# Moving every float32r operand of a two-layer block from 192 to 128 modulo 512 bytes of SBUF

## The chip, the cores and the metric

The kernel runs on one core of one Trainium2 chip. The metric is the device time of one execution in microseconds, as the median of several runs. A core has a matrix engine (TensorE, PE in the profile, its weight loads PEld), a vector engine (VectorE, DVE), a scalar engine (ScalarE, ACT), GpSimd (POOL) and SyncE (SP), which here only issues DMAs. Data lives in SBUF, a memory of 128 partitions; an address below is a byte offset inside a partition, the same in all 128. Matmul results go to PSUM.

## What is computed

Two transformer layers over one sequence of 512 tokens and 1024 features, all in float32. Layer 0 mixes tokens with HGRN2 (a gated linear recurrence in chunks), layer 1 with three groups of dilated window attention; each mixer is followed by a SwiGLU network with 2816 hidden features. Six modulation vectors a layer come from a small condition `c`.

```python
def reference(x, c, positions, ada_w, ada_b, norm_g, hgrn_w_in, ...):
    cond = jax.nn.silu(c)
    ...
    h = x
    for layer in range(DEPTH):
        mod = (cond @ ada_w[layer] + ada_b[layer])[:, None, :]
        sh1, sc1, g1, sh2, sc2, g2 = jnp.split(mod, 6, axis=-1)
        u = rms_norm(h, norm_g[layer, 0]) * (1.0 + sc1) + sh1
        ...
            y = hgrn2_mixer(u, ...) or dilated_attention_mixer(u, ...)
        h = h + (1.0 + g1) * rms_norm(y, norm_g[layer, 1])
        u = rms_norm(h, norm_g[layer, 2]) * (1.0 + sc2) + sh2
        y = swiglu_ffn(u, ffn_w_in[layer], ffn_w_out[layer])
        h = h + (1.0 + g2) * rms_norm(y, norm_g[layer, 3])
    return h
```

## The kernel before

**Float32 from three float32r products.** The kernel computes its large products with operands of the type float32r. It splits each operand `a` of a large product into a high part (`hi`, a cast to float32r, on ScalarE) and a low part (`lo` = `a` - `hi`, on VectorE), and sums three products. That is the helper `three`, whose three lines carry nearly all matmuls of the profile:

```python
def three(ps, ah, al, bh, bl, start, stop):
    pe.matmul(ps, ah, bh, start=start, stop=False)   # L431
    pe.matmul(ps, ah, bl, start=False, stop=False)   # L432
    pe.matmul(ps, al, bh, start=False, stop=stop)    # L433
```

The first operand is stationary (128 x 128, loaded by a LDWEIGHTS ahead of each matmul), the second is the moving one (128 partitions x 512 or 256 columns). In a row of the profile `out<-a,b` has the moving operand as `a` and the stationary one as `b`.

**Weights.** The class `Stream` brings weight tiles of 128 x 2048 floats from HBM (`raw`, two buffers, DMAs on SyncE's queue) and splits them into `hi` and `lo` (three buffers each; `hiq` and `loq` are the same places under another name).

**Where float32r operands stand in SBUF.** Tiles are taken from pools that are stacked from the left end or from the right end of SBUF, in the order in which the pools open. `base`, the first pool from the left, holds `h`, `ident`, `ones`, `shared` and, at its end, `uh` and `ul`, the two parts of the normed activations. Then come `raw`, `hi` and `lo`. All of `uh`, `ul`, `raw`, `hi` and `lo` start at 192 modulo 512 bytes, and every slice that a matmul takes of them begins at a multiple of 512 bytes from there. Three groups of tiles in later pools are brought to a place by a pad tile that nothing reads or writes: `apart` (attention's reordered activations, left) by 96 floats and `oh` of the mixers' outputs (right) by 72 floats, both to 192 modulo 512; and `th`, `tl` by 112 floats. The last two lie behind the two `spare` tiles, which start at 192 and are 6144 bytes long each, so 12288 + 448 bytes further: at 128 modulo 512. The first products' two `late` tiles, from the right, lie at 448. `oT`, whose places also serve as `ol`, and the FFN's `oh` and `ol` lie at 192.

**The stages**, in the order of time (us of the span): modulation and the value product of HGRN, 0 to 77; HGRN heads with their gates, to 265; its output product and the turn into the FFN, to 344; FFN of layer 0, to about 695 (plain blocks, then `seven_products`, then the output product); attention with `seven_values`, to about 1130; its output product and the turn, to 1202; FFN of layer 1, to the end.

`seven_products` computes the FFN's input product of one block of 128 hidden features (gate and up together) with seven block products instead of eight, Strassen's scheme. Each of the seven (`run`) is 4 x 3 matmuls of 256 columns; three take slices of `uh` and `ul` as the moving operand, four take slices of `th` and `tl`, which hold sums and differences of such slices. There are 16 blocks in layer 0 and 18 in layer 1. `seven_values` does the same for four attention value products, with the activations stationary and `hiq`, `loq` moving. `block` is the plain form (24 matmuls of 512 columns, or, in the turns, two halves of 256).

The order of instructions on each engine is written out by hand around the turns and in the seven products; elsewhere a scheduler orders them. Attention's small matmuls (`qk`, `ident`, `V`, `state` and the like) read float32 operands.

Of the kernel before, what the change touches and what calls it, by code (L numbers as in the profile page):

```python
# [9 lines left out]
F32 = mybir.dt.float32  # L10
# [5 lines left out]
P = 128  # L16
# [138 lines left out]
def block_kernel(tc, x, c, positions, ada_w, ada_b, norm_g, hgrn_w_in, lower, hgrn_norm_g, hgrn_w_out,  # L155
# [6 lines left out]
    R4 = lambda a: a.rearrange("p (r l) -> p l r", r=4)  # L162

    with ExitStack() as ctx:
        base = ctx.enter_context(tc.tile_pool(name="base", bufs=1))
        wp = ctx.enter_context(tc.tile_pool(name="weights", bufs=1))
        psum = ctx.enter_context(tc.tile_pool(name="psum", bufs=1, space=bass.MemoryType.PSUM))
        dpool = ctx.enter_context(tc.tile_pool(name="scratch", bufs=1, space=bass.MemoryType.DRAM))
# [6 lines left out]
        def fresh(p, shape, tag, bufs=1, dt=F32):  # L175
            uid[0] += 1
            return p.tile(shape, dt, name=f"{tag}{uid[0]}", tag=tag, bufs=bufs)
# [257 lines left out]
        def block(whi, wlo, c0, width, ps=None, tok=slice(0, S), kts=range(KT), u=(uh, ul)):  # L435

            ps = bank("mm") if ps is None else ps
            for kt in kts:
                a = kt * width + c0
                three(ps[:, tok], whi[:, a:a + P], wlo[:, a:a + P], u[0][:, kt, tok], u[1][:, kt, tok], kt == 0, kt == KT - 1)  # L440
            return ps
# [304 lines left out]
        def token_sums(th, tl, room, uh=uh, ul=ul):  # L746


            q = lambda a, k: a[:, k // 2 * 4:k // 2 * 4 + 4, k % 2 * 256:k % 2 * 256 + 256].bitcast(F32)
            t = [room[:, 2 * k:2 * k + 2].rearrange("p a (b n) -> p (a b) n", b=2) for k in range(4)]  # L750
            for k in (0, 1, 3, 2):
                dve.tensor_add(t[k], q(uh, k), q(ul, k))
            dve.tensor_sub(t[0], t[0], t[1])
            dve.tensor_sub(t[1], t[3], t[1])
            dve.scalar_tensor_tensor(t[3], t[0], -1.0, t[3], op0=OP.mult, op1=OP.subtract)
            dve.scalar_tensor_tensor(t[2], t[3], -1.0, t[2], op0=OP.mult, op1=OP.subtract)

            def cut():
                for k in (3, 0, 2, 1):
                    act.copy(th[:, k], t[k])  # L760
                    dve.tensor_sub(tl[:, k], t[k], th[:, k].bitcast(F32))
            return cut
# [132 lines left out]
        def ffn(l, first, close, nxt, side):  # L895
            turns.close()
            close()
            with ExitStack() as fx:
# [4 lines left out]
                with ExitStack() as qx:  # L903
                    sgp = qx.enter_context(tc.tile_pool(name=f"sg{l}", bufs=1, side=side))
                    qp = qx.enter_context(tc.tile_pool(name=f"quarters{l}", bufs=1, side=bass.opposite_side(side)))
                    spare = [qp.tile([P, 3 * 512], F32R, name=f"spare{l}{k}") for k in range(2)]
                    qp.tile([P, 112], F32, name=f"pad_q{l}")
                    th = qp.tile([P, 4, 4, 256], F32R, name=f"th{l}")
                    tl = qp.tile([P, 4, 4, 256], F32R, name=f"tl{l}")
                    for j in range(PLAIN[l]):  # L910
                        if j == 0:
                            pss = first
                        else:
                            pss = []
                            for i in range(2):
                                w = st.take()
                                pss += [block(*w, k * P, 256) for k in range(2)]
                        sg = [fresh(sgp, [P, S], "sg", 2) for _ in range(2)]
                        for k in range(2):
                            act.activation(sg[k], pss[k], AF.Silu)  # L920
                        if j == 0:
                            cut = token_sums(th, tl, midt[:, NF - 8:])
                        for k in range(2):
                            dve.tensor_mul(mid(2 * j + k), pss[2 + k], sg[k])
                        if j == 0:
                            cut()
                            fixed.close()
                    seven_products(range(2 * PLAIN[l], NF), mid, sgp, spare, th, tl)
# [415 lines left out]
        qp = cx.enter_context(tc.tile_pool(name="h_q", bufs=1))  # L1344
# [268 lines left out]
        def open_attention():  # L1613
# [20 lines left out]
            return v_prod  # L1634

        ffn(0, first, h0.close, ((1, 0), open_attention), "right")
        v_away = dpool.tile([P, NT, 512], F32, name="v_away")

# [195 lines left out]
        for kind, g, i in order:  # L1834
# [22 lines left out]
            for k in range(2):  # L1857
# [9 lines left out]
                7: [back(3)]}  # L1867
        first = mixer_out(oT, store[0], (3, 5), gates.pop((1, 2)), 1, "left", cx.close, tail)
        ffn(1, first, hx.close, None, "right")


# [29 lines left out]
```

## Time and profile before

| | |
|---|---|
| median of 3 runs | 1519.1 us (1518.32 to 1520.51) |
| profiled execution, its own time | 1520.42 us |
| its span, first to last instruction | 1518.7 us |
| granted TensorE clock | 0.997 |
| busy: PE, PEld, DVE, ACT, POOL | 99%, 87%, 70%, 47%, 15% |
| moved by DMA | 199.14 MB, mean 131 GB/s |
| matmuls | 9231 |

Matmuls are pipelined: one starts before the one ahead of it has ended, so their durations overlap, and the ends are modelled. The spacing of their starts, read from the timeline, is what each one costs in a train without gaps. Busy shares count overlapped time once.

### The profile page before, as it was taken

Reading aid. Unit: us, or ns where it says so; the run is one execution under the profiler, and the core shown is the slowest. Engines: PE = TensorE matmul, PEld = TensorE weight load, DVE = VectorE, ACT = ScalarE, POOL = GpSimd, SP = SyncE. Lnnn points to the kernel's source line nnn. Section 1 sums busy time; section 2 is a strip of 40 time slices with the busy share of each in tenths; the row PEclk is TensorE's granted clock in tenths of the full one; section 3 lists DMA queues with packets and bytes.
Section 4 is the critical chain, followed back from the end, with each engine's and each line's share of the span. In section 5 each row is a group of like instructions: output and inputs, shape, how many; then the busy total and the mean of one; then the engine's idle time right before and its main releaser. Section 6 shows DMA issues by size and latency. Waiting matters only on the chain. (4 is left out here: it accounts for less than half of the span.)

```text
span 1518.7 us, 23536 instructions
## 1 busy us (share of the span) xinstructions
PE 1501.0 (99%) x9231; PEld 1316.2 (87%) x9231; DVE 1061.3 (70%) x1837; ACT 719.0 (47%) x1215; POOL 235.2 (15%) x208
## 2 busy tenths in 40 slices
PE   8999999999999999999999999999999999999998
PEld 6777888898999988888987888988888899999886
DVE  4577767486888897476667766686466978888633
ACT  4433443363454433375545666356655544454231
POOL 1012211031222211140001110011002212221100
PEclk9999999999999999999999999999999999999999
DMA  9554444125333356423166540365213333334521
GB/s 308 171 175 132 160 139 167 56 84 166 112 106 104 106 196 227 152 103 125 57 194 169 149 129 29 116 190 140 83 53 116 102 94 111 112 105 147 199 106 56
DMA packets 206943, 199.14 MB, mean 131 GB/s; under 512 B 6840, under 2 KB 164720, under 8 KB 206576
## 3 DMA queue, kind: packets, MB, share of 16 engines
q1 hardware_dynamic: 203856, 190.87, 40.7%
q10 hardware_dynamic: 1952, 6.65, 1.2%
q8 instruction: 72, 1.18, 0.3%
q0 software_dynamic: 1024, 0.13, 0.2%
q14 instruction: 39, 0.32, 0.1%
HBM read 192.31 MB, written 5.31 MB: 130 GB/s over the span
## 5 line engine op out<-in xcount | busy, mean ns | idle before, releaser
L88 DVE TENSOR_TENSOR lo<-raw,hi 128x2048 fp32r<-128x2048 f32 x68 | 158.8, 2336 | 94.3 <-ACT hi L87 94.1
L87 ACT CAST hi<-raw 128x2048 fp32r<-128x2048 f32 x68 | 129.8, 1908 | 193.6 <-DMA raw<-in_ffn_w_out_dram 55.6
L431 PE MATMUL ps_mm<-apart,hi 128*128 128x512 f32 x384 | 151.4, 394 | 0.0
L432 PE MATMUL ps_mm<-apart,hi 128*128 128x512 f32 x384 | 151.2, 394 | 0.0
L433 PE MATMUL ps_mm<-apart,lo 128*128 128x512 f32 x384 | 150.7, 394 | 0.0
L431 PE MATMUL ps_mm<-uh,hi 128*128 128x512 f32 (+1 forms) x400 | 146.3, 366 | 0.0
L432 PE MATMUL ps_mm<-ul,hi 128*128 128x512 f32 (+1 forms) x400 | 144.3, 361 | 1.0 <-DVE ul L531 1.0
L433 PE MATMUL ps_mm<-uh,lo 128*128 128x512 f32 (+1 forms) x400 | 144.5, 361 | 0.0
L814 ACT CAST hiq<-raw 128x1024 fp32r<-128x1024 f32 x68 | 68.4, 1051 | 66.1 <-DVE raw L802 65.1
L431 PE MATMUL ps_mm<-hi,oh 128*128 128x512 f32 x240 | 94.0, 392 | 0.0
L432 PE MATMUL ps_mm<-lo,oh 128*128 128x512 f32 x240 | 93.4, 389 | 0.0
L431 PEld LDWEIGHTS ps_mm<-uh,hi 128*128 128x128 f32 x400 | 75.5, 189 | 19.7 <-issue 8.4
L432 PEld LDWEIGHTS ps_mm<-ul,hi 128*128 128x128 f32 x400 | 75.6, 189 | 12.1 <-DVE ul L531 1.4
L433 PEld LDWEIGHTS ps_mm<-uh,lo 128*128 128x128 f32 x400 | 75.5, 189 | 11.5
L433 PEld LDWEIGHTS ps_mm<-apart,lo 128*128 128x128 f32 x384 | 72.2, 188 | 14.9 <-DVE lo L88 0.3
L432 PEld LDWEIGHTS ps_mm<-apart,hi 128*128 128x128 f32 x384 | 72.2, 188 | 14.2
L431 PEld LDWEIGHTS ps_mm<-apart,hi 128*128 128x128 f32 x384 | 72.2, 188 | 14.0
L250 DVE SCALAR_TENSOR_TENSOR shared<-raw,cond,shared 128x512 f32<-128x512 f32 x98 | 73.3, 748 | 10.6 <-DMA raw<-in_ada_w_dram 9.7
L818 DVE TENSOR_TENSOR loq<-raw,hiq 128x1024 fp32r<-128x1024 f32 x68 | 80.0, 1218 | 0.4 <-ACT hiq L814 0.4
L252 POOL PARTITION_ALL_REDUCE shared<-shared x14 | 45.9, 3280 | 203.5 <-DVE shared L250 203.5
L798 POOL TENSOR_TENSOR raw<-raw 128x512 f32<-128x512 f32 x34 | 54.6, 1607 | 104.5 <-DVE loq L794 47.3
L802 DVE TENSOR_TENSOR raw<-raw 128x1024 f32<-128x1024 f32 x34 | 41.7, 1226 | 39.1 <-POOL raw L798 39.1
(448 smaller groups left out, 4393.9 us busy)
## 6 DMA issues: line engine op xcount, KB each, us to landing
raw<-in_ada_w_dram SPq DMA_DIRECT2D x40, 1024.0 KB, 5.2
raw<-in_ffn_w_in_dram SPq DMA_DIRECT2D x136, 256.0 KB, 3.6
raw<-in_attn_w_in_dram SPq DMA_DIRECT2D x48, 512.0 KB, 5.3
raw<-in_ffn_w_out_dram SPq DMA_DIRECT2D x22, 1024.0 KB, 4.9
raw<-in_hgrn_w_in_dram SPq DMA_DIRECT2D x12, 1024.0 KB, 5.5
raw<-in_attn_w_in_dram SPq DMA_DIRECT2D x12, 1024.0 KB, 5.2
raw<-in_ffn_w_in_dram SPq DMA_DIRECT2D x10, 1024.0 KB, 5.1
first<-in_ada_w_dram SPq DMA_DIRECT2D x14, 512.0 KB, 7.4
```

Source lines behind the costliest of these rows:

```text
L87: self.nc.scalar.copy(hi, t)
L88: self.nc.vector.tensor_sub(lo, t, hi.bitcast(F32))
L250: dve.scalar_tensor_tensor(a, r[:, k], sc, a, op0=OP.mult, op1=OP.add)
L252: pool.partition_all_reduce(a, a, P, bass.bass_isa.ReduceOp.add)
L431: pe.matmul(ps, ah, bh, start=start, stop=False)
L432: pe.matmul(ps, ah, bl, start=False, stop=False)
L433: pe.matmul(ps, al, bh, start=False, stop=stop)
L798: pool.tensor_add(r[:, 2], r[:, 2], r[:, 0])
L802: dve.tensor_tensor(r[:, 0:2], r[:, 0:3:2], r[:, 1:2].broadcast_to((P, 2, 512)), op=OP.add)
L814: act.copy(hi, src)
L818: dve.tensor_sub(lo, src, hi.bitcast(F32))
```

## The change

Two pads are added and one grows. `shift_r` (16 floats, 64 bytes) is the first tile from the right end, so every tile of the right stack moves down by 64 bytes. `shift_l` (112 floats, 448 bytes) is the first tile of `base`, so every tile of the left stack moves up by 448 bytes. Both are -64 modulo 512. `pad_q` grows from 112 to 128 floats, so that `th` and `tl` move up by 512 bytes and stay at 128 modulo 512. The stationary and the moving operands of all float32r matmuls then start at 128 modulo 512, with the two `late` tiles at 384. Float32 tiles and the targets of the DMAs move along. No instruction is added, taken away or moved.

```diff
     with ExitStack() as ctx:
+        ctx.enter_context(tc.tile_pool(name="shift", bufs=1, side="right")).tile([P, 16], F32, name="shift_r")
         base = ctx.enter_context(tc.tile_pool(name="base", bufs=1))
+        base.tile([P, 112], F32, name="shift_l")
         wp = ctx.enter_context(tc.tile_pool(name="weights", bufs=1))
...
                     spare = [qp.tile([P, 3 * 512], F32R, name=f"spare{l}{k}") for k in range(2)]
-                    qp.tile([P, 112], F32, name=f"pad_q{l}")
+                    qp.tile([P, 128], F32, name=f"pad_q{l}")
                     th = qp.tile([P, 4, 4, 256], F32R, name=f"th{l}")
                     tl = qp.tile([P, 4, 4, 256], F32R, name=f"tl{l}")
```

## The prediction

> **What bounds the kernel.** I read the page's busy lines and its slices first, then the waits of TensorE.
>
> ```profile
> span 1518.7 us, 23536 instructions
> PE 1501.0 (99%) x9231; PEld 1316.2 (87%) x9231; DVE 1061.3 (70%) x1837; ACT 719.0 (47%) x1215; POOL 235.2 (15%) x208
> PEclk9999999999999999999999999999999999999999
> ```
> ```profile
> PE ps_mm L1128 <- DVE cols L1158: 1.9, 1, 1.9
> PE ps_b L1819 <- ACT h L1797: 1.5, 2, 1.1
> PE ps_b L1212 <- POOL expo L195: 1.2, 1, 1.2
> PE ps_b L512 <- DVE xn L506: 1.2, 2, 0.6
> ```
>
> TensorE is busy for 99% of the span at the full granted clock, and its worst wait in the whole program is 1.9 us. (Columns of the second view: total us, times, longest.) So the program lasts as long as its matmuls take to follow each other, and a change that touches no instruction can only matter through that spacing. The durations do not show it, since matmuls overlap; the starts do. Here are the first and the last row of three unbroken trains, from the timeline (start us, duration us, line, tiles).
>
> ```profile
> 1402.97 0.39 PE L433 MATMUL ps_b<-hi,ol 128*128 128x512 f32 x1
> ...
> 1494.09 0.39 PE L433 MATMUL ps_a<-hi,ol 128*128 128x512 f32 x1
> ```
> ```profile
> 317.78 0.28 PE L431 MATMUL ps_mm<-uh,hi 128*128 128x256 f32 x1
> ...
> 319.22 0.28 PE L431 MATMUL ps_mm<-uh,hi 128*128 128x256 f32 x1
> ```
> ```profile
> 387.59 0.28 PE L431 MATMUL ps_mm<-th,hiq 128*128 128x256 f32 x1
> ...
> 390.99 0.28 PE L431 MATMUL ps_mm<-th,hiq 128*128 128x256 f32 x1
> ```
>
> The tile behind the arrow that comes first is the moving operand, the second the stationary one. Between the two rows lie 402, 12 and 30 matmuls. Spacing: 91.12 us / 402 = 226.7 ns for 512 columns; 1.44 / 12 = 120.0 ns for 256 columns of `uh`; 3.40 / 30 = 113.3 ns for 256 columns of `th`. From the first two, 256 columns cost 226.7 - 120.0 = 106.7 ns, and a fixed 13.3 ns comes on top of every matmul whose moving operand lies at 192. For `th` and `tl` the fixed part is 113.3 - 106.7 = 6.7 ns. These two are the only float32r tiles that lie at 128 modulo 512 already (448 bytes behind `spare`, which lies at 192). Their stationary operands lie at 192, as everywhere. The difference is not in one train only:
>
> ```profile
> L431 PEld LDWEIGHTS ps_mm<-th,hiq x204: 187/188/192, 387.1 to 1380.7; 128*128 128x128 f32 x102
> L431 PE MATMUL ps_mm<-th,hiq x204: 276/276/286, 387.2 to 1380.8; 128*128 128x256 f32 x102
> L431 PEld LDWEIGHTS ps_mm<-uh,spare x136: 187/192/192, 382.8 to 1376.5; 128*128 128x128 f32 x136
> L431 PE MATMUL ps_mm<-uh,spare x136: 278/283/283, 383.0 to 1376.7; 128*128 128x256 f32 x136
> L431 PE MATMUL ps_mm<-hiq,uh x96: 282/283/365, 739.5 to 989.3; 128*128 128x256 f32 x96
> L1190 PE MATMUL ps_mm<-late,uh x16: 389/389/397, 60.0 to 74.5; 128*128 128x512 f32 x16
> ```
>
> (Durations are least/median/greatest, by tile.) In every train a duration is the spacing plus 163 ns: 276 for `th`, 283 for `uh`, and 283 again where `hiq` moves, whose slices follow each other in the tile exactly as those of `th` do. So the walk through the tile is not what sets `th` apart; the start address is what is left. `late` lies at 448, and its 389 ns are the 0.39 of the train at 192.
>
> **The change, part by part.** Counts are from the loops. With 512 columns: 192 (first values) + 576 (24 blocks of HGRN) + 2x192 (both mixers' outputs) + 288 (12 plain FFN blocks) + 2x528 (FFN outputs) + 192 (two value products) + 1152 (48 query and key blocks) = 3840. With 256 columns at 192: 34x36 in the seven products, 4x168 in the seven values, 384 halves = 2280. With 256 columns at 128 (`th`, `tl`): 34x48 = 1632.
>
> 1. The left pad (448 bytes) lifts every left tile, the right pad (64 bytes) lowers every right tile: modulo 512 each falls by 64. No instruction is added, removed or moved, on any engine or queue; the pads are never read or written. Cost of the pads themselves: 0 of time and 576 bytes of room with the next item. The tightest place is in the FFN, where `tl` ends 864 bytes below `sg`; 288 are left, so no new pair of tiles shares bytes there.
> 2. `pad_q` grows by 64 bytes, so that `th` and `tl` stay at 128 while all else comes down to them. For them only the distance to their stationary operand changes, from -64 to 0.
> 3. Moving operands go from 192 to 128. I take the fixed part of `th`: 13.3 to 6.7 ns. 512 columns: 3840 x 6.67 = 25.6 us. 256 columns: 2280 x 6.67 = 15.2 us. `th`: 0. Together -40.8 us. The bounds are below and above nothing: if the distance of the two operands is what counts, this term is 0 and item 2 costs 1632 x 6.67 = +10.9; if the fixed part falls to what the half-rate float32 matmuls pay, it is larger. Their row:
>
> ```profile
> L1725 PE MATMUL ps_a<-qk,qk 128*128 128x256 f32 x48 | 11.7, 380 | 0.0
> ```
>
> 380 - 163 = 217 ns for 256 columns at twice 106.7, a fixed part of about 4 ns. From 6.7 to 4 on all 7752 matmuls would be another 21 us, -62 in all. I take -40.8, because `th` is the same engine mode, width and stationary tile.
> 4. Stationary operands also go from 192 to 128. No row shows a float32r load from another offset. The loads of `th` and of `uh` come from the same tiles and take 188 and 192 ns, 4 ns apart, so I take 0; the ends are those of item 3.
> 5. Float32 operands (`h`, `ident`, `qk`, `V`) move too, by 64 bytes. I take 0: the two groups below read `ident` and `h` at 128 and `qk` at 320, and their means lie 1 ns apart.
> ```profile
> L1792 PE MATMUL ps_a<-ident,h 128*128 128x128 f32 x120 | 18.4, 274 | 0.7 <-DVE h L1780 0.7
> L1743 PE MATMUL ps_a<-qk,qk 128*128 128x128 f32 x128 | 17.0, 275 | 0.2 <-DVE h L1799 0.2
> ```
>
> 6. ScalarE, VectorE and the DMAs write the moved tiles. The nearest rows write the same shape to 128 (`th`) and to 192 (`hiq`): 1045 and 1052 ns on ScalarE. That is 0.7% of an engine that is 47% busy: 0. Of the DMAs no row compares two offsets; TensorE's waits above name none of them, so 0 again.
>
> ```profile
> L760 ACT CAST th<-mid x8: 1041/1045/1053, 344.4 to 1202.1; 128x1024 fp32r<-128x1024 f32 x8
> L814 ACT CAST hiq<-raw x68: 1041/1052/1060, 378.3 to 1379.3; 128x1024 fp32r<-128x1024 f32 x68
> ```
>
> What can be late once TensorE is faster? By stage (us, PE, PEld, DVE, ACT busy, counts in brackets):
>
> ```profile
> 0.00:90.00 90.00, 85.31 (x485) 63.99 (x486) 45.35 (x90) 40.40 (x60) 5.85 (x16) 0.96 0.79 235
> 380.00:530.00 150.00, 150.00 (x1280) 149.46 (x1280) 126.91 (x137) 71.75 (x91) 34.86 (x30) 1.00 0.37 106
> 820.00:1140.00 320.00, 317.50 (x1786) 275.69 (x1787) 210.51 (x617) 185.56 (x379) 34.28 (x33) 1.00 0.40 116
> ```
>
> In the seven products one column block takes 36 x 120.0 + 48 x 113.3 = 9760 ns; it would take 84 x 113.3 = 9520, and VectorE needs 126.91/150 of 9760 = 8260. It stays covered. In attention VectorE has 66%. In the first 90 us the DMAs are 79% busy and other waits set the pace: I count the 192 matmuls there as lost, 1.3 us. Around the four turns between mixer and FFN, TensorE waits for `xn` and the like, through short chains that do not run through its own matmuls; some 200 matmuls a turn, half of their gain lost, is 4 x 200 x 6.67 / 2 = 2.7 us. Hence -40.8 + 1.3 + 2.7 = -36.8. The profiled execution took 1520.4 us (its span 1518.7), 1.3 above the median of the runs, 1519.1. Sum: 1520.4 - 36.8 = 1483.6, or about 1482 against that median.
>
> [...]
>
> **Rivals.**
> - *Distance, not place.* The stream of the moving operand and the load of the next stationary one run at the same time and get in each other's way when they start at the same offset; `th` is fast because it lies 64 bytes below its weights. Then all else keeps 13.3 ns, `th` and `tl` go from 6.7 to 13.3, and the kernel becomes slower by 1632 x 6.67 = 10.9 us: 1530. It decides once the distance explains four fifths of the effect (40.8 / (40.8 + 10.9) = 0.79). For it: the load takes 192 ns beside `uh`, 188 beside `th`. Against it: a matmul without any load beside it is no shorter.
>
> ```profile
> 87.94 0.39 PE L432 MATMUL ps_mm<-ul,hi 128*128 128x512 f32 x1
> 87.94 0.19 PEld L433 LDWEIGHTS ps_mm<-uh,lo 128*128 128x128 f32 x1
> 88.16 0.39 PE L433 MATMUL ps_mm<-uh,lo 128*128 128x512 f32 x1
> 88.48 0.16 PEld L228 LDWEIGHTS ps_mm<-raw,cond_tiles 128*32 128x32 f32 x8 [0.35 <-issue]
> ```
>
>   The matmul at 87.94 has a load beside it from its start, that at 88.16 none for 320 ns; both last 0.39. Without the 13.3 ns the second would show 0.38. Ends of matmuls are modelled, so this is no proof.
> - *Only the narrow ones.* The 13.3 ns of 512 columns is due to something else, only 256 columns gain: -15.2 us, 1504. For it: no 512-column row at 128 exists. Against: the fixed part is the same for both widths at 192.
> - *More falls away.* Aligned loads as well: -62 us, 1457.
> [...]
>
> **How the numbers follow.** Chances: the forecast 0.60 with a range of its own of 1474 to 1490 (all 40.8 us gained, or a further 8 lost to waits); only the narrow 0.08; more 0.06; nothing 0.12; distance 0.14. The range 1468 to 1523 leaves out "more" and "distance", 0.20. About 0.2%, 3 us, can be told from no change here; faster 0.60 + 0.08 + 0.06 = 0.74, same 0.12, slower 0.14.
>
> **What would show it.** Right: 512-column trains at 220.0 ns spacing (duration 382 to 383), `uh` with 256 columns at 113.3 (276), `th` still 276, loads at 188 beside all of them, the seven products at 9.52 us a block, TensorE still 98 to 99% busy. Wrong: `th` at 283 and 389 unchanged (distance), 389 unchanged with 276 everywhere (only the narrow), or the spacing as forecast but TensorE idle for much more than the 17.7 us of now (1518.7 - 1501.0).

## The result, and the profile after

The changed kernel takes 1529.0 us (1528.4 to 1531.5), against 1519.1 before: ratio 1.0067, 95% interval 1.0050 to 1.0084. It became slower by about 10 us where 37 us less were forecast. The rival "distance, not place" had named 1530. The profiled execution took 1528.4 us.

The page's busy lines and one window in the seven products of layer 0 (us, then PE, PEld, DVE, ACT, POOL busy, counts in brackets):

```profile
span 1526.7 us, 23536 instructions
PE 1510.1 (99%) x9231; PEld 1326.0 (87%) x9231; DVE 1064.4 (70%) x1837; ACT 718.4 (47%) x1215; POOL 235.1 (15%) x208
```
```profile
380.00:530.00 150.00, 150.00 (x1246) 149.73 (x1245) 123.34 (x133) 68.78 (x87) 34.30 (x29) 1.00 0.37 106
```

TensorE is as busy as before and waits for nothing new; its longest wait is 2.0 us, at the same place. But the 150 us of the window now hold 1246 matmuls where there were 1280, at the same granted clock of 1.00. 150/1246 is 120.4 ns a matmul, 150/1280 was 117.2. The lines by tile say which ones became slower (least/median/greatest ns):

```profile
L433 PEld LDWEIGHTS ps_mm<-th,hiq x204: 192/192/192, 385.7 to 1388.2; 128*128 128x128 f32 x102
L433 PE MATMUL ps_mm<-th,hiq x204: 283/283/283, 385.8 to 1388.4; 128*128 128x256 f32 x102
L433 PE MATMUL ps_mm<-uh,spare x136: 278/283/284, 381.5 to 1384.0; 128*128 128x256 f32 x136
L433 PE MATMUL ps_mm<-hiq,uh x96: 282/283/365, 743.1 to 992.1; 128*128 128x256 f32 x96
```

`uh` and `hiq` moved from 192 to 128 and kept their 283 ns. `th` stayed at 128 and went from 276 to 283, its load from 188 to 192, without the least spread. The starts agree (timeline; from the first row to the second it is 35, 23 and 402 matmuls):

```profile
385.84 0.28 PE L433 MATMUL ps_mm<-th,hiq 128*128 128x256 f32 x1
...
390.04 0.28 PE L435 MATMUL ps_mm<-th,loq 128*128 128x256 f32 x1
```
```profile
390.16 0.28 PE L433 MATMUL ps_mm<-uh,hiq 128*128 128x256 f32 x1
...
392.92 0.28 PE L435 MATMUL ps_a<-uh,loq 128*128 128x256 f32 x1
```
```profile
1410.92 0.39 PE L435 MATMUL ps_b<-hi,ol 128*128 128x512 f32 x1
...
1502.04 0.39 PE L435 MATMUL ps_a<-hi,ol 128*128 128x512 f32 x1
```

4.20/35 = 120.0 ns for `th` (113.3 before), 2.76/23 = 120.0 for `uh` (120.0 before), 91.12/402 = 226.7 for 512 columns (226.7 before). A block of the seven products takes 10.08 us from its start to the next where it took 9.76; for 34 blocks that is 10.9 us. Summed over the whole trace, from each start to the next, the float32r matmuls of 256 columns take 474.5 us where they took 463.7, those of 512 columns 896.2 where they took 897.7. That is +10.8 and -1.6 (with rounding) of the span's +7.9; the last -1.3 lies among the float32 matmuls and the waits. Of the +10.8, `th` and `tl` have 9.6; the rest is `uh` and the others.

### The profile page after: what moved, and what is told of

Read it like the earlier page. It is cut to its first block, busy times and chain, and to the rows that moved or that the text cites. A ratio compares the mean times of both kernels' runs of the same rounds, so it can differ in the third digit from the quotient of the medians.

```text
span 1526.7 us, 23536 instructions
## 1 busy us (share of the span) xinstructions
PE 1510.1 (99%) x9231; PEld 1326.0 (87%) x9231; DVE 1064.4 (70%) x1837; ACT 718.4 (47%) x1215; POOL 235.1 (15%) x208
## 5 line engine op out<-in xcount | busy, mean ns | idle before, releaser
L433 PEld LDWEIGHTS ps_mm<-apart,hi 128*128 128x128 f32 x384 | 72.2, 188 | 14.1
```

## The experiments

**Place or distance.** In the kernel before, `th` differs from `uh` in two things: its place (128, not 192) and its distance from its weights (-64 bytes, not 0). The change took the place to all and the distance from `th`. Two kernels part them. The first is the changed kernel with the old `pad_q`: all operands at 128, `th` and `tl` at 64.

```diff
-                    qp.tile([P, 128], F32, name=f"pad_q{l}")
+                    qp.tile([P, 112], F32, name=f"pad_q{l}")
```

> The changed kernel with the pad of th and tl back at 112 floats: th and tl at 64, everything else float32r at 128 modulo 512. Distance theory (what counts is the start of the moving operand minus that of the stationary operand being loaded beside it): the distance is -64 again, th at 276 ns duration and 113.3 ns spacing, 1519 us, the same as before. Place theory (a moving operand at 128 is fast only against loads at 192, or a multiple of 128 bytes is what helps): 64 is no such place, th stays at 283 ns, 1529 us.

Measured: 1519.7 us, ratio to before 0.9995 (0.9987 to 1.0004). `th` is fast again, at 64:

```profile
L433 PE MATMUL ps_mm<-th,hiq x204: 276/276/286, 385.8 to 1380.0; 128*128 128x256 f32 x102
```

The second is the kernel before with the new `pad_q` and nothing else: `th` and `tl` at 192 like their weights.

```diff
-                    qp.tile([P, 112], F32, name=f"pad_q{l}")
+                    qp.tile([P, 128], F32, name=f"pad_q{l}")
```

> The kernel before with the pad of th and tl alone grown from 112 to 128 floats: th and tl at 192, distance 0, nothing else moved. Distance theory: the whole loss of the change comes back, th at 283 ns, 1632 x 6.67 = 10.9 us more, 1529 us. If the loss came from the shift of the other tiles (float32 operands, DMA targets, writes of the other engines): 1519 to 1522 us.

Measured: 1531.5 us, ratio 1.0073 (1.0060 to 1.0086).

```profile
L431 PE MATMUL ps_mm<-th,hiq x204: 283/283/315, 386.5 to 1390.4; 128*128 128x256 f32 x102
```

The whole loss is in the 16 floats added to `pad_q`. The two big pads, which move everything else, do nothing that can be measured. Place is ruled out.

**What a distance costs.** The next kernel holds nothing but trains of 72 matmuls, the moving operand at every 16 bytes (512 columns: every 32) from 256 below to 256 above its stationary one; the granted clock is 1.0.

> Matmuls alone, in trains of 72, that compute no part of the reference: float32r, 256 and 512 moving columns, the stationary operand at 0 modulo 512 and the moving one at each distance from -256 to +256 in steps of 16 bytes (32 for 512 columns). Distance theory: 283 and 389 ns at 0 and at +-256 (late against uh), 276 and 382 at -64; the other distances are open, and one value for both widths at each distance is expected. If only the narrow ones can gain, wide trains stand at 389 at every distance.

The groups of this kernel, by train (busy us, mean ns of one). A train's spacing is its busy time less one duration, over 71; the starts, from the 21st on, give the figure to 0.1 ns.

```profile
L49 PE MATMUL wide_m000above<-M,W 128*128 128x512 f32 x72 | 16.5, 389 | 0.0
L49 PE MATMUL wide_m064above<-M,W 128*128 128x512 f32 x72 | 16.6, 391 | 0.0
L49 PE MATMUL wide_m064below<-M,W 128*128 128x512 f32 x72 | 17.0, 395 | 0.0
L49 PE MATMUL narrow_m000above<-M,W 128*128 128x256 f32 x72 | 8.8, 283 | 0.0
L49 PE MATMUL narrow_m064above<-M,W 128*128 128x256 f32 x72 | 8.3, 276 | 0.0
L49 PE MATMUL narrow_m064below<-M,W 128*128 128x256 f32 x72 | 8.6, 281 | 0.0
L49 PE MATMUL narrow_m192below<-M,W 128*128 128x256 f32 x72 | 8.3, 276 | 0.0
```

By the starts: 256 columns take 120.0 ns at distance 0, 113.3 at +64 and +112, 117.8 at -64, and 116.7 to 120 elsewhere. 512 columns take 226.7 at 0, 228.9 at +64 and 233 to 234 at the others tried; that they would have one value with the narrow ones at each distance was wrong. The pattern repeats every 256 bytes (-192 is +64). So distance 0 is among the worst for narrow matmuls and the best for wide ones. 226.7 is exactly twice 113.3: per column the wide ones had the narrow ones' best rate all along, and at no distance tried do they get the 25.6 us of the forecast.

**Places again, and the size of the load.** The same trains with the pair at six places, then with fewer stationary columns, and with distances that differ for a matmul's own and for the next stationary operand.

> Matmuls alone, no part of the reference. (a) The stationary operand at 64, 96, 128, 192, 256 and 320 modulo 512, with the moving one at the same offset and 64 bytes below. Distance theory: 283 and 276 ns (narrow), 389 and 382 (wide) at every place; place theory: the times differ by place. (b) Stationary operands of 96, 64 and 32 columns: if the load and the stream collide, a shorter load costs less at distance 0; if the 13.3 ns belong to the stream alone, it stays. (c) Two places in turn, so that a matmul's distance to its own stationary operand and to the next one, which is loaded beside it, differ. If the next one counts: nextbelow 276, nextsame 283; if its own counts, ownbelow 276 and ownsame 283.

```profile
L63 PE MATMUL narrow_w128at_same<-M,W 128*128 128x256 f32 x72 | 8.8, 283 | 0.0
L63 PE MATMUL narrow_w192at_same<-M,W 128*128 128x256 f32 x72 | 8.8, 283 | 0.0
L63 PE MATMUL narrow_nextsame<-M,W 128*128 128x256 f32 x72 | 8.8, 283 | 0.0
L63 PE MATMUL narrow_nextbelow<-M,W 128*128 128x256 f32 x72 | 8.6, 280 | 0.0
L63 PE MATMUL narrow_l032cols_same<-M,W 128*32 128x256 f32 x72 | 8.3, 276 | 0.0
L63 PE MATMUL wide_l032cols_same<-M,W 128*32 128x512 f32 x72 | 16.8, 394 | 0.0
```

At offsets of 64, 96, 128, 192, 256 and 320 bytes in the tiles the spacings are the same to 0.02 ns. A load of 32 columns in place of 128 takes the narrow train at distance 0 from 120.0 to 113.3. The sizes between follow no simple rule, though: 96 columns give 116.0, 64 columns 120.0 again, and the wide train at distance 0 becomes slower with each smaller load (230.0, 230.0 and 231.7 where 128 columns gave 226.7). So the size of the load matters, but "a shorter load costs less" is not what the trains show. Where the distance to the next weights is always 0, whatever that to a matmul's own (`nextsame`), the narrow train takes 119.9; where that to the next is always -64 (`nextbelow`), 117.8; where its own is always 0 and the next is not (`ownsame`), 116.6. This points to the load of the next weights, which runs beside the stream (PEld is busy for 475.8 us of this kernel's span of 589.1, PE for 571.8). It isn't a proof for both widths: wide trains with the next always at 0 took 233.3, not 226.7. The size of that load changes the narrow spacing by up to 6.7 ns, and where it starts by 2.1 (119.9 against 117.8), so in this case the load is not free to the matmul beside it; by what means is not shown.

**The order of the operands.** In the kernel `th` at -64 had 113.3 ns, in the trains 117.8. The seven products alternate high and low tiles, so trains in their order (`kk`) were tried, and repeats of -64 behind other trains (`h`).

> Trains of 72 float32r matmuls by themselves; nothing of the reference is computed. Open from the two micro kernels before: at a distance of -64 bytes a train of 256 columns came at 117.8 ns, but th and tl in the kernel at 113.3. Theory A (the order of the operands counts): the trains marked kk use the order of the seven products (weights high, high, low; moving high, low, high) and come to 113.3 ns at -64, those with only one of the two orders (kt: weights, tk: moving) show which. Theory B (what ran before counts): h1 to h6 repeat -64 behind other trains and differ by more than 1 ns among themselves, kk stays at 117.8. At distance 0 both say 120.0 narrow and 226.7 wide in any order. Wide at odd multiples of 16 bytes: by the period of 256 bytes and the rows so far, 229 to 234 ns, none under 226.7. Other widths at distance 0: if the fixed part is one sixteenth of the stream rounded to 6.67 ns, 384 columns take 173.3, 128 columns 60.0.

```profile
L79 PE MATMUL narrow_kk_m064below<-M,W 128*128 128x256 f32 x72 | 8.6, 281 | 0.0
L79 PE MATMUL narrow_kk_m000above<-M,W 128*128 128x256 f32 x72 | 8.8, 283 | 0.0
L79 PE MATMUL narrow_h_m064below<-M,W 128*128 128x256 f32 x288 | 33.2, 276 | 0.0
```

The order does nothing (117.8 in all three). But the four trains at -64 further on (x288) ran at 113.3: one distance has two steady spacings. At +64 the same train took 117.8 here and 113.3 in the first train kernel. This kernel also answers for other sizes (distances 0, +64 and -64). The least spacings by the starts:

```profile
L79 PE MATMUL c320wide_m000above<-M,W 128*128 128x320 f32 x72 | 10.7, 309 | 0.0
L79 PE MATMUL c384wide_m000above<-M,W 128*128 128x384 f32 x72 | 12.6, 334 | 0.0
L79 PE MATMUL c448wide_m064above<-M,W 128*128 128x448 f32 x72 | 14.6, 362 | 0.0
```

146.7, 173.3 and 200.0 ns for 320, 384 and 448 columns. With 113.3 for 256 and 226.7 for 512 that is 113.3 per 256 columns, rounded up to a multiple of 6.67 ns. It is just as well 106.7 per 256 columns with 13.3 on top for 320 to 512 columns and 6.7 for 256; these widths can't tell the two readings apart. 128 and 192 columns both take 111.7, not the 60.0 expected for 128; 512 columns at odd multiples of 16 bytes take 230 to 235.

**The weights 64 bytes higher, in the kernel.** A check of the wide column of the table.

```diff
         wp = ctx.enter_context(tc.tile_pool(name="weights", bufs=1))
+        wp.tile([P, 16], F32, name="shift_w")
+        ctx.enter_context(tc.tile_pool(name="shift", bufs=1)).tile([P, 112], F32, name="shift_back")
```

> The kernel before with all of the weights' tiles 64 bytes higher (192 to 256 modulo 512) and all else where it was. Counted by the operands: 512 columns, 2016 matmuls at -64 and 1776 at +64 (0 before); 256 columns, 1200 at -64 (0 before), 672 at +64 (0 before), 1428 of th and tl at -128 (-64 before). Theory distance, with the spacings of the trains: wide 2016 x 6.7 + 1776 x 2.2 = +17.4 us; narrow 672 x -6.67 = -4.5, 1428 x +5.3 = +7.5, 1200 x -2.2 (or -6.67) = -2.7 (-8.0): together +17.8 or +12.5, so 1532 to 1537, with the 512-column rows (uh and hi, apart and hi) at 392 to 400 in place of 389. Rival of the prediction (operands that start alike cost 6.7 ns at every width): all wide ones gain, 3792 x -6.7 = -25 us, under 1500. Rival place: 1519.

Measured: 1529.0 us, ratio 1.0061 (1.0045 to 1.0076), some 9 us slower; the direction that the distances say, but less than the 12.5 to 17.8. The rows by tile (389 was the median of each before):

```profile
L433 PE MATMUL ps_mm<-apart,hi x384: 390/394/580, 712.1 to 1115.8; 128*128 128x512 f32 x192
L434 PE MATMUL ps_b<-lo,oh x88: 392/392/394, 545.2 to 1519.6; 128*128 128x512 f32 x88
```

The starts give on average 233.3 ns at -64 and 229.1 at +64, as in the trains, and 14.1 us more for the 3710 wide matmuls that the next one follows within 270 ns in both kernels (17.4 expected for all). The other 130 wide ones took 3.6 us less, the float32 matmuls and the waits 2.8 less: TensorE is idle for 15.7 us (1526.8 - 1511.1) in place of 17.7. The narrow ones came to +0.3 together, one of the two sums expected, but not by the expected parts (+64 took 117.8, not 113.3).

**A better distance for `uh` in the seven products.** The weights of three of the seven runs (R: B11, T4, B21) get places inside their tiles: 48, 576 and 1104 floats (`Q3` is that strided view). The `spare` tiles grow to 1632 floats, and the pads behind them keep all else where it was. The wide ones keep distance 0.

```diff
-                    act.copy(places(i)[0][0][:, 0:1536], raw[i][:, 512:])
+                    act.copy(Q3(places(i)[0][0]), Q4(raw[i])[:, 1:4])
...
-                run(half(0, 0), R, 0, B11)
-                run(half(3, 1), R, 512, T4)
-                run(half(1, 0), R, 1024, B21)
+                run(half(0, 0), R, 48, B11)
+                run(half(3, 1), R, 48 + 528, T4)
+                run(half(1, 0), R, 48 + 2 * 528, B21)
```

> The kernel before, with the three parts of the weights R in the seven products at 48, 576 and 1104 floats of their tiles in place of 0, 512 and 1024: uh then lies 64 bytes above its weights in the first product (B11), 64 below in the third (B21), th stays 64 below (T4); every other pair stays as before, the moving operands do not move. Theory distance: B11's 12 matmuls of a block come at 113.3 ns as at +64 in the trains, B21's at 113.3 (as th) or 117.8 (as the train at -64): 34 x 24 x 6.67 = 5.4 us less, 1513.7, or 34 x (12 x 6.67 + 12 x 2.2) = 3.6 less, 1515.5. Rival place: no moving operand leaves 192, so 1519.1. Rival room: the copies in three strided parts take longer on ScalarE and VectorE and delay a block: above 1520.

Measured: 1518.1 us, ratio 0.9987 (0.9979 to 0.9996), some 2 us less where 3.6 to 5.4 were expected. First the kernel before: the first matmul of T4, B21 and t2 of one block (timeline). T4 takes 1.38/12 = 115.0 ns, B21 1.42/12 = 118.3.

```profile
413.71 0.29 PE L431 MATMUL ps_b<-th,hiq 128*128 128x256 f32 x1
...
415.09 0.28 PE L431 MATMUL ps_b<-uh,hiq 128*128 128x256 f32 x1
...
416.51 0.29 PE L431 MATMUL ps_b<-th,hiq 128*128 128x256 f32 x1
```

Then this one: the first matmul of B11, T4, B21, the three runs t2, T3, t1, and B22:

```profile
411.08 0.28 PE L431 MATMUL ps_a<-uh,hiq 128*128 128x256 f32 x1
...
412.44 0.28 PE L431 MATMUL ps_b<-th,hiq 128*128 128x256 f32 x1
...
413.86 0.28 PE L431 MATMUL ps_b<-uh,hiq 128*128 128x256 f32 x1
...
415.28 0.29 PE L431 MATMUL ps_b<-th,hiq 128*128 128x256 f32 x1
...
419.38 0.28 PE L431 MATMUL ps_b<-uh,hiq 128*128 128x256 f32 x1
```

B11 at +64 takes 1.36/12 = 113.3 ns. T4, with operands 64 bytes apart as before, takes 1.42/12, and B21 the same (118.1 and 117.9 by the starts in ns), the last three 4.10/36 = 113.9. Beside before's 120.0, 114.9 and 118.4 for the first three, T4 loses half of what B11 gains and B21 gains 0.5: T4's own distance is the old one, but the run ahead of it now lies at +64. A block takes 9.71 us in place of 9.76, 1.6 us less in 34 blocks. The copies into three strided parts take no longer than the plain ones: 1481 ns on ScalarE and 1751 on VectorE, 1482 and 1751 before.

**What ran before.** Trains at -64 behind others, and blocks of seven runs with these distances.

> Trains of 72 float32r matmuls by themselves; nothing of the reference is computed. The trains before showed two steady spacings at one and the same distance of -64 bytes (117.8 ns, and 113.3 behind some other trains). Theory 'history': the state in which a train arrives decides; a train of 256 columns at -64 keeps 113.3 behind a narrow train at distance 0 (as th in the kernel behind uh) and 117.8 behind a wide one, and steadily the same over all 72. At +64 likewise one of the two. In the blocks of seven runs of 12 (blocks_before has the distances of the kernel before, blocks_mixed those with R at 48, 576 and 1104, blocks_below those with R at 16, 576 and 1104), 84 matmuls take 84 x 113.3 + 36 x 6.7 = 9.76 us in blocks_before and 9.60 in blocks_below. Rival 'the tile's place or a number of trains': the spacing at -64 doesn't go by what ran ahead of it, and blocks_below is as slow as blocks_before.

```profile
L58 PE MATMUL narrow_behind_same<-M,W 128*128 128x256 f32 x72 | 8.3, 276 | 0.0
L58 PE MATMUL narrow_behind_widesame<-M,W 128*128 128x256 f32 x72 | 8.6, 281 | 0.0
L58 PE MATMUL narrow_behind_widebelow<-M,W 128*128 128x256 f32 x72 | 8.3, 276 | 0.0
L58 PE MATMUL narrow_behind_wideabove<-M,W 128*128 128x256 f32 x72 | 8.6, 281 | 0.0
```

After its first few matmuls the same train holds 113.3 or 117.8 ns to its end, by what ran ahead of it. It isn't "117.8 behind a wide one": behind wide at -64 it is 113.3. At +64 the train took 117.8 behind all four others tried. The blocks came out as expected, 9.76 us with before's distances and 9.60 with R below. In these blocks it is the moving operand that steps, though; in the kernel it is the weights, and the blocks with the distances of the kernel above took 9.91 us here and 9.71 there.

**All of R below.** R at 16, 576 and 1104 floats (with two copies each on ScalarE and VectorE), so that no run at +64 comes in between.

```diff
+            Q2 = lambda a: a[:, 576:1632].rearrange("p (q c) -> p q c", c=528)[:, :, 0:512]
...
-                run(half(0, 0), R, 48, B11)
+                run(half(0, 0), R, 16, B11)
```

> The kernel before with the three parts of R in the seven products at 16, 576 and 1104 floats of their tiles (two copies each in place of one on ScalarE and VectorE), so that B11, T4, B21, t2, T3 and t1 all lie 64 bytes below their weights; nothing else moves. Theory (distance, with history): no run at +64 comes in between, so all 72 matmuls of a block that lie at -64 stay at 113.3 ns: 34 x 24 x 6.67 = 5.4 us less than before, 1513.7; the rows of uh and spare at 276 in place of 283. Rival: -64 settles at 117.8 as in the kernel with 48, 576, 1104: 24 x 34 x 2.2 - 48 x 34 x 4.4 = +5.4, slower than before at 1524. [...]

Measured: 1519.0 us, ratio 0.9994 (0.9985 to 1.0003): no change that can be told. The first three runs of a block:

```profile
413.47 0.28 PE L431 MATMUL ps_a<-uh,hiq 128*128 128x256 f32 x1
...
414.89 0.29 PE L431 MATMUL ps_b<-th,hiq 128*128 128x256 f32 x1
...
416.27 0.28 PE L431 MATMUL ps_b<-uh,hiq 128*128 128x256 f32 x1
...
417.68 0.29 PE L431 MATMUL ps_b<-th,hiq 128*128 128x256 f32 x1
```

118.0, 115.2 and 117.5 ns by the starts in ns: three runs at one distance, two spacings. T4 settles at 113.3 (115.2 with the first few); into it both operands step down by 64. B11 and B21 stay near 117.8; into them the weights, or both operands, step up by 64 (all modulo 256). So the first theory of the expectation fell, and its rival held for two runs of the six. A delay by the second copies would fit the time as well (they add 0.19 us on ScalarE, 623 + 1049 ns against 1482, and 0.15 on VectorE, 685 + 1218 against 1751), but not the trace: all 34 blocks run without a gap, at 9.73 us in place of 9.76. That is 1.1 us in all, too little to tell in the whole time.

**The steps into the runs.** Fifteen blocks at the kernels' true places and in other orders.

> Blocks of 84 float32r matmuls of 256 columns by themselves, in runs of 12 at the places of the seven products; nothing of the reference is computed. Which of the two spacings a run at -64 or +64 takes (113.3 or 117.8) seemed to go by the step into it: in the kernels with R moved, 113.3 where the moving operand or both step down by 64 bytes or the weights step down, 117.8 where the weights step up by 64 or both step up. Theory 'step': kernel_before, kernel_mixed and kernel_below repeat the kernels' runs to 0.5 ns (second to fourth run 113.3/120/113.3, 117.8/117.8/113.3, 113.3/117.8/113.3), so that some other order of the runs, to be read here, has all six at 113.3: 9.57 us a block against 9.74 in kernel_before. Rival: something that the trains lack (uh's own strides, the banks of sums) chooses the spacing, and the three kernels' blocks are not repeated.

```profile
L63 PE MATMUL kernel_before_b<-M,W 128*128 128x256 f32 x84 | 9.9, 279 | 0.0
L63 PE MATMUL th_above_b<-M,W 128*128 128x256 f32 x84 | 10.2, 281 | 0.0
L63 PE MATMUL one_same_above_b<-M,W 128*128 128x256 f32 x84 | 9.8, 278 | 0.0
```

The blocks of the three kernels come out as in the kernels, run by run, to 0.3 ns (before: 120.0, 114.9, 118.4, then 113.8 over three, 118.4). So distance and the steps between them are enough, and the strides of `uh` or the PSUM banks aren't needed. Start to start, a block takes 9.76 us as before, 9.71 and 9.73 in the two kernels with R moved, 9.68 in the best order and 9.99 with `th` above its weights. No order tried had all six runs at 113.3; the second half of the expectation was wrong.

**The best order, in the kernel.** R at 48 (B11, +64), 576 (T4, -64) and 1088 (B21, 0); B21 ahead of T4.

```diff
-                run(half(0, 0), R, 0, B11)
-                run(half(3, 1), R, 512, T4)
-                run(half(1, 0), R, 1024, B21)
+                run(half(0, 0), R, 48, B11)
+                run(half(1, 0), R, 1088, B21)
+                run(half(3, 1), R, 576, T4)
```

> The kernel before with R's parts at 48 (B11), 576 (T4) and 1088 (B21) floats of their tiles and the runs in the order B11, B21, T4, t2, T3, t1, B22: B11 lies at +64, B21 and B22 at 0, all of th and tl at -64. The trains of these places took 9.68 us a block against 9.76 for the kernel before's. Theory (the spacing of a run is set by its distance and the step into it, and nothing else decides): 34 x 0.08 = 2.8 us less, ratio 0.998, with runs of 12 at 113.3, 119.9, 114.9, 113.3, 113.3, 113.3, 118.4 ns. Rival: the new order or the second copy on ScalarE and VectorE delays a block: 1519 or more.

Measured: 1516.9 us against 1519.4 in the same series, ratio 0.9982 (0.9974 to 0.9991), 2.5 us less where 2.8 were expected. The 34 blocks take 2.6 us less by their starts. B11, B21, the four runs of `th`, B22:

```profile
410.49 0.28 PE L431 MATMUL ps_a<-uh,hiq 128*128 128x256 f32 x1
...
411.85 0.28 PE L431 MATMUL ps_b<-uh,hiq 128*128 128x256 f32 x1
...
413.29 0.29 PE L431 MATMUL ps_b<-th,hiq 128*128 128x256 f32 x1
...
418.75 0.28 PE L431 MATMUL ps_b<-uh,hiq 128*128 128x256 f32 x1
```

1.36/12 = 113.3, 1.44/12 = 120.0, 5.46/48 = 113.8. This version beats both kernels, the one before by 0.2%.

## Why the prediction was wrong

The bound was read rightly: TensorE's spacing sets the time, and nothing else moved it. Point by point:

1. The pads themselves cost nothing: right (0.9995 with the pads and the old distance).
2. `pad_q`: the text says that for `th` "only the distance to their stationary operand changes, from -64 to 0", and the sum then counts that as 0. This was the only thing in the change with an effect: 1632 x 6.67 = 10.9 us forecast by the rival, 34 x 0.32 = 10.9 in the starts of the blocks.
3. **This is the step that failed.** It took 13.3 ns of every spacing as a fixed part that hangs on the moving operand's place, for both widths, and that falls to 6.7 at 128. Place changes nothing: trains take 120.0 and 226.7 ns at all six. `th` owed its 6.7 ns to the distance from its weights. And for 512 columns the 13.3 over "2 x 106.7" are what they cost at best: 226.7 is their least at every distance and with every load tried. Only the narrow train paid 6.7 ns more than it had to. The split as such agrees with the widths at distance 0 (13.3 over 106.7 per 256 columns for 256, 320, 384 and 512; 448 has 20.0); what the 13.3 depended on was assumed. Another reading was open from the prediction's own rows, since 226.7 is 2 x 113.3: `th` and the wide trains at one rate, `uh` the odd one. Of the -40.8 us the wide 25.6 were not to be had, and the narrow 15.2 need another distance, not another place.
4. Stationary operands: 0, right as to place.
5. and 6. Float32 operands and the other engines: 0, right. After the change `qk` with 256 columns still takes 380 ns, and the cast to `th` 1052 (1045 before).
The losses of cover, 1.3 and 2.7 us, had nothing left to act on. No train of 512 columns came under 226.7 ns, none of 256 under 113.3.

Against "only the narrow ones" the prediction set that the fixed part is the same for both widths at 192. That was no evidence: two trains give a slope and one fixed part only if it is taken as the same for both.

The row set "against" the rival, a matmul with no load beside it and still 0.39 us long, bore no weight for a reason that stood in its own sentence: ends are modelled. It was also a wide matmul, and no wide train, with smaller loads or at other distances, came under 226.7 ns. The rival's own row, a load of 192 ns beside `uh` and 188 beside `th`, was the better witness: after the change it is 192 beside both. The chance of 0.14 for it was too small, since `th` differs from `uh` in place and in distance, and no row told the two apart.

## What to carry to other kernels

When one group of instructions is faster than its like, list all in which it differs before its advantage is given to the others; here it differed in two things, and the change removed the one that counted. A slope and a fixed part taken from two trains don't say what the fixed part depends on; try other readings of the same rows too, here that cost goes with size (226.7 is 2 x 113.3). Where float32r matmuls of 256 columns follow each other, try the operands 64 bytes apart modulo 256 (113.3 or 117.8 ns here, against 120.0 at distance 0), and read the spacing in the kernel itself, since the order of the runs matters; leave those of 512 columns at distance 0 (226.7 ns here, 228.9 or more at every other distance tried modulo 256).

## What the runs showed of the hardware

- In these trains, with loads of 128 columns, the spacing of float32r matmuls depended on where the moving operand starts against the stationary one, modulo 256 bytes (-192 as +64), and not on where the pair lies (the same to 0.02 ns at six places). 256 columns: 113.3 to 120.0 ns; 512 columns: 226.7 to 234.7.
- Several of the steady spacings are multiples of 6.67 ns (113.3 = 17, 120.0 = 18, 226.7 = 34, 233.3 = 35); 117.8 lies between two of them.
- At -64, and at +64, two steady spacings were measured (113.3 and 117.8); the way in chose, and a train of 72 then kept it to its end. Why stays open: the trains show that the size of the load beside the stream matters, by no simple rule (113.3, 120.0, 116.0 and 120.0 ns with 32, 64, 96 and 128 columns at distance 0), and that a step of the moving operand does not act like a step of the weights (9.91 and 9.71 us a block at the same distances), but not the cause.
